# Stick-breaking attention with the keys in even and odd pairs: a scan over pairs, and the subtraction ahead of GpSimd's product

## The chip, the cores and the metric

One core of a Trainium2 chip runs the whole kernel. Its engines are TensorE (PE in the profile, PEld for its weight loads), VectorE (DVE), ScalarE (ACT), GpSimd (POOL) and SyncE (SP, which issues the DMAs here). Each has a queue of its own and they wait for each other by semaphores. The metric is the device time in microseconds of one execution; lower is better.

## The reference

A decoder layer on 2048 tokens of width 1024, in float32. The change touches the eight stick-breaking heads of 64 dimensions:

```python
for start in range(0, S, Q_BLOCK):
    end = start + Q_BLOCK
    z = jnp.einsum('bhqd,bhkd->bhqk', q[:, :, start:end], k[:, :, :end]).astype(jnp.float32) * scale
    past = jnp.arange(end)[None, :] < jnp.arange(start, end)[:, None]
    log_beta = jax.nn.log_sigmoid(z)
    log_1m = jnp.where(past, jax.nn.log_sigmoid(-z), 0.0)
    acc = lax.cumsum(log_1m, axis=3, reverse=True) - log_1m
    w = jnp.where(past, jnp.exp(log_beta + acc), 0.0)
    outs.append(jnp.einsum('bhqk,bhkd->bhqd', w.astype(v.dtype), v[:, :, :end]))
```

So the weight of key s for query t is sigmoid(z[t,s]) times the product of (1 - sigmoid(z[t,j])) over the keys j between s and t. Beside them stand four differential heads (two softmax maps each), an output projection, and a SwiGLU feed-forward layer.

## The kernel before

The kernel has three stretches: the norm of the input and the first projections (to 75 us), the attention heads with the projections of later heads between them (to 1400 us, the stick-breaking ones to about 838), and the feed-forward layer. Matmuls take their operands as a high and a low half in float16, so that most products are three matmuls.

The stick-breaking heads are worked in four groups g of two heads h. For each group, `units_sb` goes over eight pairs of query blocks s (256 queries, as two blocks a of 128 on the partitions), and for each over chunks c of 512 keys, from the diagonal one backwards, and the two heads h: 160 units in all. The first chunk of each s is diagonal, with 256 or 512 keys (32 units of each size); the other 96 units have 512 keys. `W` is a unit's number of keys.

One unit (`unit_sb`): `scores` puts z for both a into PSUM (tile `psum`, two places of 1024 floats that take turns). In `main`, ACT writes `be`, the sigmoid of z, to SBUF (L736), and then 1 - beta, the sigmoid of -z, over z in PSUM (L737). DVE runs a product from the last key to the first over it, one scan for each a, into `gp` (L742); it starts at 2^14 on the diagonal and elsewhere at the first element of the `gp` of the chunk before, that is `cx[h]`. One small reduce (L746) copies that start value to the end of `gp`; on the diagonal a memset (L741) puts it there. POOL then multiplies `be` by `gp` shifted by one key (L754, on the diagonal L751): these are the weights. Two units later ACT casts them to float16 (`high`, tile `wh`, L762), three units later DVE subtracts to get the low half (`low`, tile `wl`, L769), both are turned by DMA transposes, and five units after the h = 1 unit `values` multiplies with V.

The main loop sets the order, by a clock of ticks, one tick for each unit:

```python
for kind in ("", "main", "mid", None):
    main() if kind == "main" else clock.run(kind)
```

What is due under "" runs ahead of the unit's `main` (here: `low` of the unit three before, and `values`), "mid" behind it (the evacuations of projections, `evac_q`, `evac_k`, `evac_v`), and None takes the rest ("hi": the casts of ACT). `look_ahead` then issues the next unit's scores and `fill_next` a piece of a projection.

`be`, `gp` and other tiles come from one ring of seven buffers (`ppp`, by `ptile`): a new tile takes the place of the one seven allocations ago and its first writer waits for that one's last reader. Before, each unit takes two, `gp` and then `be`.

Of the kernel before, what the change touches and what calls it, by code (L numbers as in the profile page):

```python
# [64 lines left out]
def hybrid_layer_kernel(  # L65
# [6 lines left out]
    nc = tc.nc  # L72
# [152 lines left out]
    with ExitStack() as actx:  # L225
# [49 lines left out]
        def ptile(name):  # L275
            return ppp.tile([128, 1026], F32, tag="pp", name=name)

# [3 lines left out]
        def transposed(wh, w):  # L281
# [3 lines left out]

        lam_t = rtp.tile([128, 1024], F32, tag="rt", name="lam_t")[:, 0:256].rearrange(
            "p (i d) -> p i d", i=4)
        subg = small("subg", bufs=1)

        def load_constants():  # L290
            nc.gpsimd.dma_start(out=mask_b, in_=mask_in.rearrange("m p k -> p m k"))
            for i, l in enumerate((lambda_q1, lambda_k1, lambda_q2, lambda_k2)):
                nc.sync.dma_start(out=lam_t[:, i, :], in_=l.to_broadcast([128, 64]))
            nc.sync.dma_start(out=subg, in_=diff_subln_g.rearrange("o p -> p o"))
            nc.sync.dma_start(out=qkg[:, 0, :], in_=diff_q_norm_g.to_broadcast([128, 64]))
            nc.sync.dma_start(out=qkg[:, 1, :], in_=diff_k_norm_g.to_broadcast([128, 64]))
# [196 lines left out]

        def stack(ps, dst, ts):

            for a, m in ((0, 0), (64, 1)):
                nc.scalar.activation(dst[a:a + 64, m, ts], ps[a:a + 64, :], AF.Copy, scale=OUT_SC)
            for a, m in ((0, 0), (64, 1)):
                nc.vector.scalar_tensor_tensor(dst[64 - a:128 - a, m, ts], ps[a:a + 64, :], OUT_SC,
                                               dst[a:a + 64, m, ts], ALU.mult, ALU.subtract)  # L500

        def evac_q(ps, q, ts):
            stack(ps, q[:, 0], ts)
            if ts.stop == 512:
                clock.at(1, lambda: swap(q))
# [4 lines left out]

        evac_k = stack

        def project_sb(c, g):
# [7 lines left out]
            for w2, ev, dst in ((ws[0], evac_q, q), (ws[1], evac_k, k)):  # L521
                for u in range(2):
                    yield from bank_totals()
                    ps = pj_tile("pj")
                    ts = slice(u * 256, u * 256 + 256)
# [6 lines left out]
                    clock.at(1, lambda ps=ps, ev=ev, dst=dst, ts=ts: ev(ps, dst, ts), "mid")  # L532
# [180 lines left out]
        def unit_sb(g, s, c, h, cx, step):  # L713
# [3 lines left out]
            u = {}  # L717

            def scores():
                need(g, cd)  # L720
                q, k = qkv[g][cd][0], qkv[g][c][1]
                z = u["z"] = place("z", 1024).rearrange("p (a n) -> p a n", a=2)
                for a in range(2):
                    qs = o + a * 128
                    for y in range(2):
                        mm(z[:, a, 0:W], q[:, y, h, qs:qs + 128], k[:, h, 0:W], y == 0,
                           y == 1 and not diag)
                    if diag:
                        mm(z[:, a, qs:qs + 128], ident_b, mask_b[:, 0, :], False, True)

            def main():
                z, sc = u["z"], scl[g]
                gp = ptile("gp").rearrange("p (a n) -> p a n", a=2)
                be = ptile("be")[:, 0:2 * W].rearrange("p (a n) -> p a n", a=2)

                nc.scalar.activation(be, z[:, :, 0:W], AF.Sigmoid, scale=sc[:, 0:1])  # L736
                nc.scalar.activation(z[:, :, 0:W], z[:, :, 0:W], AF.Sigmoid, scale=sc[:, 1:2])  # L737
                for a in range(2):
                    e = o + (a + 1) * 128 if diag else 512
                    if diag:  # L740
                        nc.vector.memset(gp[:, a, e:e + 1], 2.0 ** 14)  # L741
                    nc.vector.tensor_tensor_scan(  # L742
                        gp[:, a, 0:e][:, ::-1], z[:, a, 0:e][:, ::-1], be[:, a, 0:e][:, ::-1],
                        2.0 ** 14 if diag else cx[h][:, a, 0:1], ALU.mult, ALU.bypass)
                if not diag:
                    nc.vector.tensor_reduce(gp[:, :, 512], cx[h][:, :, 0:1], axis=AX.X, op=ALU.max)  # L746
                cx[h] = gp
                if diag:
                    for a in range(2):
                        e = o + (a + 1) * 128  # L750
                        nc.gpsimd.tensor_mul(be[:, a, 0:e], be[:, a, 0:e], gp[:, a, 1:e + 1])  # L751
                    nc.gpsimd.memset(be[:, 0, o + 128:W], 0.0)
                else:
                    nc.gpsimd.tensor_mul(be, be, gp[:, :, 1:513])  # L754

# [3 lines left out]
                def high():  # L759
                    wh = u["wh"] = htile("wh")[:, 0:n]  # L760
                    if True:
                        nc.scalar.copy(wh, b2)  # L762
# [49 lines left out]
        def unit_diff(g, i, m, j, cx):  # L812
# [6 lines left out]
            def scores():  # L819
# [4 lines left out]
                for o in range(b, e, 512):  # L824
# [887 lines left out]
```

## Time and profile before

| | |
|---|---|
| time of the runs, median of 3 | 2962.2 us (2958.57 to 2964.27) |
| the profiled execution's own time | 2957.14 us |
| its span | 2955.1 us |
| mean TensorE clock granted | 0.948 |
| busy: PE, DVE, ACT, POOL | 2578.5, 2465.3, 1534.1, 1482.8 us |

A row of a group gives the line, the engine, the operation, output and inputs by the program's names, the shape, and the count; then the busy time in us and the mean of one in ns; then the idle time of the engine just before these instructions, and who ended most of it. A row of a timeline gives the start and the duration in us. A row of the waits gives who waited for whom, the sum in us, how often, and the longest.

### The profile page before, as it was taken

Reading aid. Unit: us, or ns where it says so; the run is one execution under the profiler, and the core shown is the slowest. Engines: PE = TensorE matmul, PEld = TensorE weight load, DVE = VectorE, ACT = ScalarE, POOL = GpSimd, SP = SyncE. Lnnn points to the kernel's source line nnn. Section 1 sums busy time; section 2 is a strip of 40 time slices with the busy share of each in tenths; the row PEclk is TensorE's granted clock in tenths of the full one; section 3 lists DMA queues with packets and bytes.
Section 4 is the critical chain, followed back from the end, with each engine's and each line's share of the span. In section 5 each row is a group of like instructions: output and inputs, shape, how many; then the busy total and the mean of one; then the engine's idle time right before and its main releaser. Section 6 shows DMA issues by size and latency. Waiting matters only on the chain.

```text
span 2955.1 us, 51682 instructions
## 1 busy us (share of the span) xinstructions
PE 2578.5 (87%) x20076; PEld 1587.4 (54%) x20076; DVE 2465.3 (83%) x3653; ACT 1534.1 (52%) x2539; POOL 1482.8 (50%) x1259
## 2 busy tenths in 40 slices
PE   7867778879678687786899899989999999999999
PEld 6646556657466576675674344444444444444444
DVE  7998999999988889989756788889877776777776
ACT  6776777777545565555534545454444343334332
POOL 2453455455757757666313455655454444444442
PEclk8989989989889899997999999999999999999999
DMA  4565667677655545567865412231116432112111
GB/s 162 103 130 107 123 128 130 124 127 133 108 99 95 93 97 98 108 117 154 178 158 142 136 58 79 84 113 68 43 62 127 138 102 86 43 43 78 52 43 72
DMA packets 736790, 305.80 MB, mean 103 GB/s; under 512 B 619296, under 2 KB 713760, under 8 KB 736544
## 3 DMA queue, kind: packets, MB, share of 16 engines
q1 hardware_dynamic: 736272, 302.43, 45.3%
q8 instruction: 157, 2.57, 0.4%
q14 instruction: 89, 0.73, 0.1%
q0 software_dynamic: 272, 0.07, 0.0%
HBM read 127.34 MB, written 28.31 MB: 53 GB/s over the span
## 4 chain that ended last, share of the span: by engine, by line
PE 47%; DVE 28%; issue 9%; POOL 5%; ACT 5%; DMA 4%; SPq 1%; DVEq 0%; ACTq 0%; POOLq 0%
PE pw L167 32%; PE psum L167 14%; DVE gp L742 4%; DVE wl L769 4%; DVE mx L178 2%; DVE fs L1296 2%; DVE acc_a L1569 2%; DMA wt<-wl 2%; DVE pt L178 1%; DVE hh L1348 1%; DVE wmx L105 1%; DMA wt<-al 1%; DVE rt L638 1%; DVE ws L161 1%; POOL sc L1486 1%
## 5 line engine op out<-in xcount | busy, mean ns | idle before, releaser
L167 PE MATMUL pw<-t,fs 128*128 128x512 f16 x3696 | 805.5, 380 | 12.3 <-ACT fs L1295 3.8
L167 PEld LDWEIGHTS <-fs 128*128 128x128 f16 x3696 | 359.6, 98 | 449.2 <-issue 6.8
L167 PE MATMUL psum<-k,q 128*128 128x512 f16 (+3 forms) x1280 | 339.8, 375 | 211.6 <-DVE gp L742 75.6
L167 PE MATMUL pw<-acc_b,at 128*128 128x512 f16 x2112 | 465.2, 380 | 19.4 <-DVE cg L1494 8.5
L167 PE MATMUL psum<-ws,h_hi 128*128 128x128 f16 x4096 | 386.4, 227 | 20.1 <-ACT psum L928 10.7
L167 PE MATMUL psum<-ws,h_lo 128*128 128x128 f16 x2048 | 374.7, 226 | 0.0
L167 PEld LDWEIGHTS <-h_hi 128*128 128x128 f16 x4096 | 336.3, 102 | 48.6 <-issue 29.7
L167 PEld LDWEIGHTS <-at 128*128 128x128 f16 x2112 | 206.1, 98 | 270.5 <-issue 26.5
L754 POOL TENSOR_TENSOR be<-be,gp 128x1024 f32<-128x1024 f32 x96 | 215.1, 2241 | 261.6 <-DVE gp L746 217.1
L167 PEld LDWEIGHTS <-q 128*128 128x128 f16 x1280 | 117.5, 100 | 329.9 <-issue 276.6
L1497 POOL TENSOR_TENSOR cg<-cg,cu 128x512 f32<-128x512 f32 x88 | 112.1, 1274 | 360.5 <-ACT cg L1496 341.0
L1569 DVE SCALAR_TENSOR_TENSOR acc_a<-pw,isd,acc_a 128x512 f32<-128x512 f32 x352 | 248.5, 744 | 49.3 <-PE pw L167 48.9
L1295 ACT ACTIVATE fs<-acc_b,fst 128x512 f16<-128x512 f32 x264 | 175.9, 713 | 211.2 <-POOL acc_b L1284 145.3
L1296 DVE SCALAR_TENSOR_TENSOR fs<-acc_b,fst,fs 128x512 f16<-128x512 f32 x264 | 248.3, 980 | 33.2 <-ACT fs L1295 33.1
L1486 POOL TENSOR_TENSOR sc<-sc 128x512 f32<-128x512 f32 x132 | 219.4, 1679 | 88.8 <-ACT sc L1480 88.8
L769 DVE TENSOR_TENSOR wl<-be,wh 128x1024 f16<-128x1024 f32 (+1 forms) x160 | 259.3, 1621 | 4.8 <-DMA wt<-wl 3.2
L742 DVE TENSOR_TENSOR_SCAN gp<-psum,gp,be 128x512 f32<-128x512 f32 x192 | 235.2, 1265 | 2.2 <-ACT psum L737 1.4
L736 ACT ACTIVATE be<-psum,gsc 128x1024 f32<-128x1024 f32 (+1 forms) x160 | 164.7, 1029 | 133.1 <-DVE wl L769 55.5
L167 PEld LDWEIGHTS <-h_lo 128*128 128x128 f16 x2048 | 209.3, 102 | 0.0
L1480 ACT COPY sc<-pw 128x512 f32<-128x512 f32 x176 | 100.1, 581 | 208.5 <-PE pw L167 184.7
L854 ACT ACTIVATE pt<-psum,nb,ds_sc 128x1024 f32<-128x1024 f32 (+4 forms) x192 | 183.0, 954 | 22.0 <-DVE pt L178 8.0
L178 DVE TENSOR_REDUCE mx<-psum 128x1 f32<-128x1024 f32 (+4 forms) x192 | 173.7, 905 | 24.1 <-PE psum L167 20.1
(222 smaller groups left out, 4850.2 us busy)
## 6 DMA issues: line engine op xcount, KB each, us to landing
acc_b<-in_w_gate_dram SPq DMA_DIRECT2D x22, 1024.0 KB, 5.2
acc_b<-in_w_up_dram SPq DMA_DIRECT2D x22, 1024.0 KB, 7.3
acc_b<-in_w_down_dram SPq DMA_DIRECT2D x22, 1024.0 KB, 9.1
raw<-in_w_in_dram SPq DMA_DIRECT2D x24, 512.0 KB, 4.6
xt<-in_x_dram SPq DMA_DIRECT2D x16, 512.0 KB, 5.2
raw<-in_w_o_dram SPq DMA_DIRECT2D x16, 512.0 KB, 4.2
mt<-mix_d SPq DMA_DIRECT2D x32, 256.0 KB, 3.5
out_dram<-acc_a SPq DMA_DIRECT2D x16, 512.0 KB, 2.9
```

The costliest lines, as they stand in the source:

```text
L167: nc.tensor.matmul(ps, lhsT=lhsT, rhs=rhs, start=start, stop=stop)
L178: fn(*a, **k)
L736: nc.scalar.activation(be, z[:, :, 0:W], AF.Sigmoid, scale=sc[:, 0:1])
L742: nc.vector.tensor_tensor_scan(gp[:, a, 0:e][:, ::-1], z[:, a, 0:e][:, ::-1], be[:, a, 0:e][:, ::-1], 2.0 ** 14 if diag else cx[h][:, a, 0 ...
L754: nc.gpsimd.tensor_mul(be, be, gp[:, :, 1:513])
L769: nc.vector.tensor_sub(wl, b2, u["wh"])
L854: nc.scalar.activation(pt, u["z"][:, 0:e - b], AF.Exp, scale=ds_sc, bias=nb[:, m:m + 1], accum_out=su[:, jj:jj + 1])
L1295: nc.scalar.activation(w[:, m, 0:4], src, AF.Copy, scale=sw)
L1296: nc.vector.scalar_tensor_tensor(w[:, m, 4:8], src, sw, w[:, m, 0:4], ALU.mult, ALU.subtract)
L1486: nc.gpsimd.tensor_add(s[m], s[m], y[m])
L1497: nc.gpsimd.tensor_mul(g, g, u)
L1569: nc.vector.scalar_tensor_tensor(acc[:, i, hs], ps, pr.isd, acc[:, i, hs], ALU.mult, ALU.add)
```

## The change

K's columns and V's tokens are stored so that in each chunk all even keys come first and then all odd ones (P = W/2 of each). The product of (1 - beta) over a pair is one step of a scan over P pairs, whose two multiplications take the even factor and the odd one. ACT now writes the even half of 1 - beta to `gp` in SBUF and the odd half over z in PSUM; the scan works in place in `gp`, which then holds the product at each pair's even key. For the even keys' weights the odd key's factor is still missing, so DVE multiplies the even half of `be` by the odd factors (a new instruction). POOL's product takes `gp` shifted by one pair, for both halves alike. `gp` is one buffer for the units of both heads (three allocations for two units instead of four). `low` of the unit three before gets the kind "low" and runs inside `main`, after the new product and before the reduce or memset that POOL waits for. Diagonal units work on their whole width, with masked scores giving 0 and 1, where before scans and products stopped at the diagonal and a memset on POOL cleared the rest.

```diff
         def evac_k(ps, k, u):
+            stack(ps.rearrange("p (n r) -> p r n", r=2),
+                  by_parity(k)[:, :, :, u * 128:u * 128 + 128])
...
-                    ts = slice(c * 512 + (2 * u + j) * 128, c * 512 + (2 * u + j + 1) * 128)
+                    ts = slice(c * 512 + u * 256 + j, c * 512 + u * 256 + 256, 2)
...
                     for y in range(2):
-                        mm(z[:, a, 0:W], q[:, y, h, qs:qs + 128], k[:, h, 0:W], y == 0,
+                        mm(za, q[:, y, h, qs:qs + 128], k[:, h, :, 0:P], y == 0,
                            y == 1 and not diag)
                     if diag:
-                        mm(z[:, a, qs:qs + 128], ident_b, mask_b[:, 0, :], False, True)
+                        n = 128 - 64 * a
+                        mm(za[:, :, P - n:P], ident_b, mask_p[:, :, 0:n], False, True)
 
             def main():
                 z, sc = u["z"], scl[g]
-                gp = ptile("gp").rearrange("p (a n) -> p a n", a=2)
+                if h == 0:
+                    step["gp"] = ptile("gp").rearrange("p (h a n) -> p h a n", h=2, a=2)
+                gp = step["gp"][:, h]
                 be = ptile("be")[:, 0:2 * W].rearrange("p (a n) -> p a n", a=2)
                 nc.scalar.activation(be, z[:, :, 0:W], AF.Sigmoid, scale=sc[:, 0:1])
-                nc.scalar.activation(z[:, :, 0:W], z[:, :, 0:W], AF.Sigmoid, scale=sc[:, 1:2])
+                nc.scalar.activation(gp[:, :, 0:P], z[:, :, 0:P], AF.Sigmoid, scale=sc[:, 1:2])
+                nc.scalar.activation(z[:, :, P:W], z[:, :, P:W], AF.Sigmoid, scale=sc[:, 1:2])
                 for a in range(2):
-                    e = o + (a + 1) * 128 if diag else 512
-                    if diag:
-                        nc.vector.memset(gp[:, a, e:e + 1], 2.0 ** 14)
+                    ga = gp[:, a, 0:P][:, ::-1]
                     nc.vector.tensor_tensor_scan(
-                        gp[:, a, 0:e][:, ::-1], z[:, a, 0:e][:, ::-1], be[:, a, 0:e][:, ::-1],
-                        2.0 ** 14 if diag else cx[h][:, a, 0:1], ALU.mult, ALU.bypass)
-                if not diag:
-                    nc.vector.tensor_reduce(gp[:, :, 512], cx[h][:, :, 0:1], axis=AX.X, op=ALU.max)
+                        ga, ga, z[:, a, P:W][:, ::-1],
+                        2.0 ** 14 if diag else cx[h][:, a, 0:1], ALU.mult, ALU.mult)
+                nc.vector.tensor_mul(be[:, :, 0:P], be[:, :, 0:P], z[:, :, P:W])
+                clock.run("low")
+                if diag:
+                    nc.vector.memset(gp[:, :, P:P + 1], 2.0 ** 14)
+                else:
+                    nc.vector.tensor_reduce(gp[:, :, P], cx[h][:, :, 0:1], axis=AX.X, op=ALU.max)
                 cx[h] = gp
-                if diag:
-                    for a in range(2):
-                        e = o + (a + 1) * 128
-                        nc.gpsimd.tensor_mul(be[:, a, 0:e], be[:, a, 0:e], gp[:, a, 1:e + 1])
-                    nc.gpsimd.memset(be[:, 0, o + 128:W], 0.0)
-                else:
-                    nc.gpsimd.tensor_mul(be, be, gp[:, :, 1:513])
+                b4 = be.rearrange("p a (r n) -> p a r n", r=2)
+                nc.gpsimd.tensor_mul(b4, b4, gp[:, :, 1:P + 1].rearrange(
+                    "p a (r n) -> p a r n", r=1).to_broadcast([128, 2, 2, P]))
...
-                clock.at(3, low, "")
+                clock.at(3, low, "low")
...
-                               v[:, kb, x, hh * 64:(hh + 1) * 64],
+                               v[:, vb, x, hh * 64:(hh + 1) * 64],
```

The mask is built anew: its diagonal part goes by an SP load and two DVE instructions into `mask_p`, even and odd columns apart; the differential heads keep theirs as `mask_b`.

How instructions then stand on DVE in two full units of the second group of heads (`gp`, `be`, `wh` and `wl` with the numbers of their buffers, so that the same unit can be found again; `q` and `k` are projections being evacuated; what the rows call SCALAR_TENSOR_TENSOR on `gp` are the scans, one for each a). Before:

```order
L742 SCALAR_TENSOR_TENSOR gp_2813<-psum_122,gp_2666,be_2814 128x512 x2
L746 TENSOR_REDUCE gp_2813<-gp_2666 128x2
L499 SCALAR_TENSOR_TENSOR q_2779<-psum_122,q_2779 64x256 x2
L769 TENSOR_TENSOR wl_2882<-be_2667,wh_2825 128x1024
L161 SCALAR_TENSOR_TENSOR ws_2373<-raw_2371,wsw_2660,ws_2373 128x1024
L742 SCALAR_TENSOR_TENSOR gp_2887<-psum_122,gp_2761,be_2888 128x512 x2
L746 TENSOR_REDUCE gp_2887<-gp_2761 128x2
L499 SCALAR_TENSOR_TENSOR q_2779<-psum_122,q_2779 64x256 x2
L769 TENSOR_TENSOR wl_2931<-be_2762,wh_2899 128x1024
```

The same two units in the changed kernel:

```order
L760 SCALAR_TENSOR_TENSOR gp_2764<-gp_2764,gp_2642,psum_122 128x256 x2
L763 TENSOR_TENSOR be_2818<-be_2818,psum_122 128x2x256
L784 TENSOR_TENSOR wl_2825<-be_2643,wh_2780 128x1024
L768 TENSOR_REDUCE gp_2764<-gp_2642 128x2
L505 SCALAR_TENSOR_TENSOR q_2788<-psum_122,q_2788 64x256 x2
L161 SCALAR_TENSOR_TENSOR ws_2373<-raw_2371,wsw_2669,ws_2373 128x1024
L760 SCALAR_TENSOR_TENSOR gp_2893<-gp_2893,gp_2764,psum_122 128x256 x2
L763 TENSOR_TENSOR be_2894<-be_2894,psum_122 128x2x256
L784 TENSOR_TENSOR wl_2901<-be_2671,wh_2835 128x1024
L768 TENSOR_REDUCE gp_2893<-gp_2764 128x2
```

The subtraction into `wl` has moved from behind the reduce and the evacuation to a place between the scans and the reduce, the scans are half as long, and the product into `be` is new.

On ACT, the second of these units before and after (`ws` is a weight being split; a row's brackets name the engines or DMA queues whose semaphores it waits for). Before:

```order
L762 CAST wh_2825<-be_2667 128x1024 [waits DMAHW6_49,Pool_49]
L157 ACTIVATE ws_2373<-raw_2371,wsw_2660 128x1024 [waits DMAHW0_49,DVE_49]
L736 ACTIVATE be_2888<-psum_122,gsc_136 128x1024 [waits PE_49,Activation_49]
L737 ACTIVATE psum_122<-psum_122,gsc_136 128x1024
L497 ACTIVATE q_2779<-psum_122 64x256 [waits PE_49]
```

After, with the unit that follows it (h = 1):

```order
L779 CAST wh_2835<-be_2671 128x1024 [waits DMAHW7_49,DVE_49,Pool_49]
L157 ACTIVATE ws_2373<-raw_2371,wsw_2669 128x1024 [waits DVE_49]
L755 ACTIVATE be_2894<-psum_122,gsc_137 128x1024 [waits PE_49]
L756 ACTIVATE gp_2893<-psum_122,gsc_137 128x2x256 [waits DVE_49]
L757 ACTIVATE psum_122<-psum_122,gsc_137 128x2x256 [waits Activation_49]
L503 ACTIVATE q_2788<-psum_122 64x256 [waits PE_49]
L503 ACTIVATE q_2788<-psum_122 64x256
L779 CAST wh_2911<-be_2765 128x1024 [waits DMAHW1_49,Pool_49]
L755 ACTIVATE be_2948<-psum_122,gsc_137 128x1024 [waits DVE_49,PE_49]
L756 ACTIVATE gp_2893<-psum_122,gsc_137 128x2x256
L757 ACTIVATE psum_122<-psum_122,gsc_137 128x2x256 [waits Activation_49]
```

There are three sigmoids for a unit instead of two. The even half of the h = 0 unit (`gp_2893`) waits for DVE, namely for `wl_2825` of the unit just before, which reads `be_2643`, the buffer that `gp_2893` takes; the odd half waits for ACT itself to end the even half.

More of the change, by code (lines that the diff above doesn't have):

```diff
@@ L266, in hybrid_layer_kernel @@
         ident_b = ac.tile([128, 128], BF16, name="ident_b")
-        mask_b = ac.tile([128, 2, 128], BF16, name="mask_b")
+        mask_b = ac.tile([128, 128], BF16, name="mask_b")
+        mask_p = ac.tile([128, 2, 128], BF16, name="mask_p")
         nlam = ac.tile([128, 1], F32, name="nlam")
@@ L275, in ptile @@
         def ptile(name):
-            return ppp.tile([128, 1026], F32, tag="pp", name=name)
+            return ppp.tile([128, 1028], F32, tag="pp", name=name)
         def htile(name):
@@ L284, in transposed @@
             return wt
-        lam_t = rtp.tile([128, 1024], F32, tag="rt", name="lam_t")[:, 0:256].rearrange(
-            "p (i d) -> p i d", i=4)
+        lam_t = rtp.tile([128, 1024], F32, tag="rt", name="lam_t")
+        mask_t = lam_t[:, 256:384]
+        lam_t = lam_t[:, 0:256].rearrange("p (i d) -> p i d", i=4)
         subg = small("subg", bufs=1)
         def load_constants():
-            nc.gpsimd.dma_start(out=mask_b, in_=mask_in.rearrange("m p k -> p m k"))
+            nc.gpsimd.dma_start(out=mask_b, in_=mask_in[1])
+            nc.sync.dma_start(out=mask_t, in_=mask_in[0])
             for i, l in enumerate((lambda_q1, lambda_k1, lambda_q2, lambda_k2)):
@@ L299, in constants @@
             nc.vector.tensor_copy(ident_b, ident)
+            nc.vector.memset(mask_p[:, :, 64:128], -(2.0 ** 120))
+            nc.vector.tensor_copy(mask_p[:, :, 0:64], mask_t.rearrange("p (n r) -> p r n", r=2))
             lam_s = small("lam_s", 2, bufs=1)
@@ L492, in weights, with stack, evac_q @@
                     yield END
-        def stack(ps, dst, ts):
+        def stack(ps, dst):
             for a, m in ((0, 0), (64, 1)):
-                nc.scalar.activation(dst[a:a + 64, m, ts], ps[a:a + 64, :], AF.Copy, scale=OUT_SC)
+                nc.scalar.activation(dst[a:a + 64, m], ps[a:a + 64], AF.Copy, scale=OUT_SC)
             for a, m in ((0, 0), (64, 1)):
[L499 to L504, printed above, removed]
+                nc.vector.scalar_tensor_tensor(dst[64 - a:128 - a, m], ps[a:a + 64], OUT_SC,
+                                               dst[a:a + 64, m], ALU.mult, ALU.subtract)
+        def evac_q(ps, q, u):
+            stack(ps, q[:, 0, :, u * 256:u * 256 + 256])
+            if u == 1:
                 clock.at(1, lambda: swap(q))
@@ L509, in swap, with by_parity, evac_k @@
                 nc.sync.dma_start(out=q[64 - a:128 - a, 1], in_=q[a:a + 64, 0])
-        evac_k = stack
+        def by_parity(k):
+            return k.rearrange("p m (r n) -> p m r n", r=2)
+        def evac_k(ps, k, u):
+            stack(ps.rearrange("p (n r) -> p r n", r=2),
+                  by_parity(k)[:, :, :, u * 128:u * 128 + 128])
         def project_sb(c, g):
@@ L524, in project_sb @@
                     ps = pj_tile("pj")
-                    ts = slice(u * 256, u * 256 + 256)
                     hs = slice(c * 512 + u * 256, c * 512 + u * 256 + 256)
@@ L717, in unit_sb @@
             u = {}
+            P = W // 2
             def scores():
                 need(g, cd)
-                q, k = qkv[g][cd][0], qkv[g][c][1]
+                q, k = qkv[g][cd][0], by_parity(qkv[g][c][1])
                 z = u["z"] = place("z", 1024).rearrange("p (a n) -> p a n", a=2)
@@ L800, in store @@
                 clock.at(1, lambda: store_mix(g, s * 256, 256, st))
-            return scores, None, main, W, 4 * W + 3 * W + (128 if diag else 0) * 2
+            return scores, None, main, W, 4 * W + 3 * W + (384 if diag else 0)
         def units_diff(g):
```

11 lines of the change are left out of this document (5 added, 6 removed).

## The prediction

> **What bounds the kernel now.** I read the page's head, then the busy time of one stretch, then the groups by form inside it, then the timeline of two units.
>
> ```profile
> span 2955.1 us, 51682 instructions
> ...
> DVE  7998999999988889989756788889877776777776
> ```
>
> The slices say that DVE (VectorE) is nearly always busy from the second slice to about the eleventh of 74 us each. That is where the stick-breaking units lie, by the lines of their first and last instruction:
>
> ```profile
> L742 DVE TENSOR_TENSOR_SCAN gp<-psum,be x128: 409/814/1220, 77.9 to 784.4; 128x128 f32<-128x128 f32 x32, 128x256 f32<-128x256 f32 x32, 128x384 f32<-128x384 f32 x32, 128x512 f32<-128x512 f32 x32
> L769 DVE TENSOR_TENSOR wl<-be,wh x160: 666/1226/3017, 85.2 to 838.2; 128x1024 f16<-128x1024 f32 x128, 128x512 f16<-128x512 f32 x32
> ```
>
> From 77.9 to 838 us, then; of what the diff touches, only the name of a mask is used later.
>
> ```profile
> core 0: us, PE busy (x) PEld busy (x) DVE busy (x) ACT busy (x) POOL busy (x), PEclk, DMA share, GB/s
> 75.00:833.00 758.00, 591.44 (x6038) 439.06 (x6038) 728.88 (x1026) 529.74 (x682) 380.39 (x316) 0.91 0.66 122
> ```
>
> In these 758 us DVE works 728.9: it is the bound, with 29 us to spare. PE (TensorE) has 591, ACT (ScalarE) 530, POOL (GpSimd) 380. So what DVE saves there shortens the kernel, until PE's 591 or a chain through ACT takes over. Who waits for whom agrees (the second row is the scores' group in this stretch):
>
> ```profile
> ACT be L736 <- DVE wl L769: 55.5, 35, 4.3
> L167 PE MATMUL psum<-k,q 128*128 128x512 f16 (+2 forms) x640 | 182.8, 385 | 135.9 <-DVE gp L742 75.6 <-DVE gp L746 28.9 <-DVE gp L741 28.0
> ```
>
> PE's 136 us ahead of the scores are waits for DVE to free a score buffer. What DVE spends on the 160 units (96 full ones of 512 keys against an earlier block, 32 diagonal ones of 512 and 32 of 256):
>
> ```profile
> L742 DVE TENSOR_TENSOR_SCAN gp<-psum,gp,be 128x512 f32<-128x512 f32 x192 | 235.2, 1265 | 2.2 <-ACT psum L737 1.4
> L742 DVE TENSOR_TENSOR_SCAN gp<-psum,be 128x512 f32<-128x512 f32 x32 | 38.9, 1214 | 0.0
> L742 DVE TENSOR_TENSOR_SCAN gp<-psum,be 128x384 f32<-128x384 f32 x32 | 30.4, 949 | 4.3 <-ACT psum L737 4.1
> L742 DVE TENSOR_TENSOR_SCAN gp<-psum,be 128x256 f32<-128x256 f32 x32 | 21.8, 682 | 0.0
> L742 DVE TENSOR_TENSOR_SCAN gp<-psum,be 128x128 f32<-128x128 f32 x32 | 13.4, 419 | 6.5 <-ACT psum L737 5.7
> L769 DVE TENSOR_TENSOR wl<-be,wh 128x1024 f16<-128x1024 f32 x128 | 220.0, 1719 | 4.3 <-DMA wt<-wl 3.2
> L769 DVE TENSOR_TENSOR wl<-be,wh 128x512 f16<-128x512 f32 x32 | 39.3, 1227 | 0.5
> L746 DVE TENSOR_REDUCE gp<-gp 128x2 f32<-128x2 f32 x96 | 12.3, 128 | 0.0
> L741 DVE MEMSET gp<- 128x1 f32 x128 | 7.6, 59 | 0.0
> ```
>
> Scans 339.7 us, the subtraction (`wl`) 259.3, reduces and memsets 19.9: 618.9. The other 110 us are evacuations of projections and weight work, 0.69 per unit. The subtraction's mean of 1.72 us mixes two cases, which the timeline shows (first DVE, then POOL, then ACT, of one stretch):
>
> ```profile
> 607.25 0.41 DVE L549 SCALAR_TENSOR_TENSOR v<-psum,v 128x256 f16<-128x256 f32 x1
> 607.59 2.98 DVE L769 TENSOR_TENSOR wl<-be,wh 128x1024 f16<-128x1024 f32 x1
> ...
> 614.05 0.12 DVE L746 TENSOR_REDUCE gp<-gp 128x2 f32<-128x2 f32 x1
> 614.09 1.21 DVE L769 TENSOR_TENSOR wl<-be,wh 128x1024 f16<-128x1024 f32 x1
> 615.23 2.45 DVE L742 TENSOR_TENSOR_SCAN gp<-psum,gp,be 128x512 f32<-128x512 f32 x2
> 617.60 0.12 DVE L746 TENSOR_REDUCE gp<-gp 128x2 f32<-128x2 f32 x1
> 617.64 1.21 DVE L769 TENSOR_TENSOR wl<-be,wh 128x1024 f16<-128x1024 f32 x1
> 618.77 2.45 DVE L742 TENSOR_TENSOR_SCAN gp<-psum,gp,be 128x512 f32<-128x512 f32 x2
> ```
> ```profile
> 607.48 2.00 POOL L754 TENSOR_TENSOR be<-be,gp 128x1024 f32<-128x1024 f32 x1 [3.96 <-DVE gp L746]
> 614.34 2.82 POOL L754 TENSOR_TENSOR be<-be,gp 128x1024 f32<-128x1024 f32 x1 [4.86 <-DVE gp L746]
> ```
> ```profile
> 615.40 1.11 ACT L736 ACTIVATE be<-psum,gsc 128x1024 f32<-128x1024 f32 x1 [1.69 <-DVE wl L769]
> ```
>
> The reduce lets POOL's product go, 0.2 us later. Where DVE starts the subtraction at once (614.09) it takes 1.21 us and POOL's product is stretched from 2.00 to 2.82. Where an evacuation comes between (607.25), POOL is first and the subtraction takes 2.98. So a unit with nothing beside it lasts 3.54 us (615.23 to 618.77), all DVE, and the other kind pays 1.77 more.
>
> **The change, by its parts.** *Scans.* Each covers half the elements: 256 in 64 diagonal scans and in the 192 of full units, 128 in 64. By the rows 682 ns, 682 + 51 (1265 less 1214, the price of a start value from memory) = 733, and 419: 43.6 + 140.7 + 26.8 = 211.1 us instead of 339.7, **-128.6**. This takes the second multiplication in the loop as free; between 128 and 512 elements the rows give (1214 - 419)/384 = 2.07 ns for an element. No row has a scan with two real operations. From below it can't be cheaper; from above I let it cost half a loop more, 1.04 ns, which is 256 x 0.265 + 64 x 0.133 = +76. I take 0, since today's row already pays twice what a plain product does per element (0.8 to 1.0 ns, below), and keep 76 as a rival.
>
> *A new product* on DVE, `be` (SBUF) by the odd half of the scores' buffer (PSUM), 512 elements in 128 units, 256 in 32. Nearest rows, of the same mix of memories:
>
> ```profile
> L1494 DVE TENSOR_TENSOR cg<-pw,sc 128x512 f32<-128x512 f32 x88 | 60.2, 684 | 29.2 <-POOL sc L1486 29.2
> L1018 DVE SCALAR_TENSOR_TENSOR acc_b<-psum,iso,acc_b 128x256 f32<-128x256 f32 x32 | 14.8, 481 | 21.4 <-PE psum L167 16.8 <-ACT psum L928 4.6
> ```
>
> 128 x 0.684 + 32 x 0.481 = **+103**. *The subtraction* now stands after the product and ahead of the reduce or memset that POOL waits for, so POOL has at that time only the product of the unit before, begun 0.2 us after that unit's reduce and 2.0 long. DVE reaches the subtraction two scans and a product later (1.4 + 0.65) if nothing lies between: a wait of 0.15 at most. At 1.21 and, by the shortest of the small form, about 0.67 us: 128 x 1.21 + 32 x 0.67 = 176.3, **-83**. Its ends are 0 (POOL still in the way) and -83. POOL starts 1.2 us later in a unit; its reader, the cast `wh`, comes two units on, so that is hidden. *Memsets:* 64 fewer, -3.8. Together **-112** on DVE.
>
> *ACT.* The second sigmoid becomes two, the even half into `gp`, the odd one in place and waiting for the first to end. Rows:
>
> ```profile
> L736 ACT ACTIVATE be<-psum,gsc 128x1024 f32<-128x1024 f32 x128 | 142.7, 1115 | 106.2 <-DVE wl L769 55.5 <-PE psum L167 30.4 <-POOL be L754 10.1
> L737 ACT ACTIVATE psum<-psum,gsc 128x1024 f32<-128x1024 f32 x128 | 138.6, 1083 | 0.0
> L736 ACT ACTIVATE be<-psum,gsc 128x512 f32<-128x512 f32 x32 | 22.0, 688 | 26.8 <-POOL be L754 8.8 <-PE psum L136 8.3 <-PE psum L167 7.7
> L737 ACT ACTIVATE psum<-psum,gsc 128x512 f32<-128x512 f32 x32 | 21.0, 655 | 0.0
> L762 ACT CAST wh<-be 128x1024 f16<-128x1024 f32 x128 | 133.8, 1045 | 38.0 <-DMA wt<-wh 16.4 <-DVE wl L769 12.0 <-POOL be L754 4.4
> ```
>
> 0.688 + 0.655 against 1.083: 0.26 more in 128 units, about 0.2 in 32, +40 on an engine with 228 us idle; hidden by itself. But `gp` is now ACT's output, one buffer for the two units h = 0, 1, and by the order on ACT the even half of an h = 0 unit waits for DVE's `wl` of the unit just before (its buffer is the `be` that this `wl` reads). Before, `be` too waited for a `wl` (the 55.5 us), but with two scans left to hide behind. Now: `wl` ends, 0.1 until ACT starts (615.30 to 615.40), 0.69, 0.655, 0.1 again, then the scan: 1.55 us in which DVE has the reduce (0.12) and the 0.69 of evacuations and weight work, which come unevenly (none at 614 us, 0.41 at 607); I take half the gaps as empty and half as full. A mean hole of (1.43 + 0.05)/2 = 0.74 in 64 pairs, about half that in the 16 small ones: 47 + 6 = **+53** given back. Its ends: 64 x 1.43 + 16 x 1.0 = +108, if evacuations wait too, and +10, if every gap has work. The h = 1 unit has no such wait: ACT goes on with `wh`, `be` and the halves, 3.5 us by the rows and some 3.3 with neighbours overlapping, against 3.1 on DVE (two scans, product, subtraction, reduce, also overlapping): +0.2 where no evacuation stands, +8 in 40 pairs. Against that, instructions overlap by 0.08 (the reduce lasts 0.12, and the next starts 0.04 after it) and there is one more in a unit: -13. Net **-5**.
>
> *PE.* Scores, values and projections keep their columns; masks gain 64 x 128 columns, hidden. V's tokens are taken at a step of two, so its 16 x 96 weight loads read `h` with a step. None of the rows has a strided load:
>
> ```profile
> L167 PEld LDWEIGHTS <-h_hi x1472: 95/98/152, 98.5 to 823.5; 128*128 128x128 f16 x184
> ```
>
> Ends: 0, and a load of twice the 98 ns, 1536 x 0.098 = 150 us on PE, of which 136 stand idle now. I take 0. *K's evacuation* reads PSUM at a step of two:
>
> ```profile
> L499 DVE SCALAR_TENSOR_TENSOR k<-psum,k 64x256 f16<-64x256 f32 x64 | 27.0, 422 | 3.8 <-ACT k L497 2.4
> ```
>
> Ends: 0, and twice the streamed part, (684 - 422)/256 = 1.02 ns x 256 x 64 = +17 on DVE. I take 0, the contiguous row being the only one. [...] *POOL's* broadcast product costs no more than a plain one in the nearest rows (256 elements):
>
> ```profile
> L640 POOL TENSOR_TENSOR st<-st,cs 128x256 f32<-128x256 f32 x32 | 28.5, 891 | 2.5
> L751 POOL TENSOR_TENSOR be<-be,gp 128x256 f32<-128x256 f32 x32 | 26.7, 834 | 3.7 <-DVE gp L742 2.6 <-DVE gp L741 0.2
> ```
>
> 7% of 2.0 us is 0.14, on an engine half idle. One more 64 KB load on SP and two small DVE operations in the first 75 us: under 1 us.
>
> **Sum:** -112 + 53 - 5 = -64, with 2 for leftover waits of `wl`: **-62 us**. Against the profiled execution's own time (2957.1, of which 2955.1 are its span) that is 2895; that execution is 5 below the median of the runs, 2962.2, so I forecast **2900**.
>
> **The rivals.**
> 1. *ACT and PE hold more of it.* PE's 591 us are 3.7 a unit on average, against 4.35 that DVE would then take (696/160), and where projection blocks stand close together PE is above its mean; holes add up when engines are this close. For: the stretch shrinks to 696 us under PE's 591. Against: that leaves 105 us of idle PE. With the hole at 1.2 instead of 0.74 (+32 on 64 to 80 pairs): 2935. Chance 0.17.
> 2. *The holes are filled,* evacuations falling where ACT is awaited: 53 becomes 13, 2860. Chance 0.13.
> 3. *Slower: the scan pays for its second multiplication.* +76: 2976. It decides from about 0.24 us for a 256-element scan (62 us over 256). For: its loop must now go through two multiplications. Against: 2.07 ns an element today, where the new product's neighbour needs (684 - 481)/256 = 0.8, so the loop already has a spare step. Chance 0.08. [...]
> 4. *Slower or no gain: the turn doesn't come,* POOL still holding the subtraction back, if its product grows past 3 us: the 83 stay, 2983. Chance 0.05.
> 5. *Strided weight loads at double price,* 591 + 150 = 741 us of PE in a stretch of now 758: the gain is all but eaten, 2950. For: no load here has a step. Against: nothing but that the bytes loaded are as many. Chance 0.07.
> 6. *K's read at a step at full price:* +17, 2917; it lies in the forecast's own range and 0.10 of its 0.50.
>
> **How the numbers follow.** The forecast has 0.50, with its own range 2875 to 2925. Runs of this kernel lie 5.7 us apart, so 0.2% (6 us) is about what can be told from nothing. The range takes in rival 2 and 1, K's 17 and the edge of 5, and leaves out 3 and 4 and some tails: 2852 to 2965. Faster: 0.50 + 0.13 + 0.15 of rival 1 + 0.03 of rival 5 = 0.81; no change 0.05; slower 0.14.
>
> **What would show it.** Right: 256-element scans at 0.73 us, the product at 0.68, `wl` of 1024 at 1.21 with hardly a row over 1.5, POOL's product at 2.0, and DVE idle ahead of every second unit's scan, released by ACT's odd-half sigmoid, some 50 us in all; the stretch near 696 us. Wrong: scans near 1.0 us (rival 3), `wl` still at 2 to 3 (4), loads from `h_hi` near 0.2 (5), or the hole ahead of scans near 100 us. Past 840 us nothing should move.

## The result and the profile after

The changed kernel takes 2926.98 us (median of 4 runs, 2924.35 to 2931.6) against 2960.39 before; the ratio is 0.9889 with a 95% interval of 0.987 to 0.9909. So it is faster by 33 us, where 62 were forecast, and the time lies 2 us past the end of the forecast's own range (2875 to 2925). In a later set of runs it gave 2927.99 and a ratio of 0.9898 (0.9881 to 0.9914).

The head of the page and DVE's row of the slices, after:

```profile
span 2929.8 us, 51760 instructions
...
DVE  8887888888988898899757788889877776776776
```

Almost all the nines of the first eleven slices have become eights: DVE is no longer always busy there. One row each for the stretch of the stick-breaking units, from the first scan to the last transpose of a `wl`, before and after (length, then busy time of PE, PEld, DVE, ACT and POOL):

```profile
77.90:839.50 761.60, 594.71 (x6066) 442.14 (x6065) 731.23 (x1032) 531.30 (x687) 385.16 (x318) 0.90 0.66 123
```
```profile
78.50:812.30 733.80, 591.77 (x6074) 442.45 (x6073) 623.19 (x1129) 570.95 (x847) 358.21 (x190) 0.90 0.70 127
```

DVE has 108 us less to do, and its idle time has grown from 30 (761.60 - 731.23) to 111 (733.80 - 623.19): of 108 us, 80 turned into waiting, and the stretch is 28 shorter. The rest of the gain in the medians is within what runs differ by: the profiled run, at 2931.6, is the slowest of the four.

The groups inside the stretch, after: DVE's first, then ACT's two halves and POOL's product.

```profile
L760 DVE TENSOR_TENSOR_SCAN gp<-gp,psum 128x256 f32<-128x256 f32 x256 | 173.3, 718 | 75.7 <-ACT psum L757 71.3 <-PE psum L167 2.8
L784 DVE TENSOR_TENSOR wl<-be,wh 128x1024 f16<-128x1024 f32 x128 | 163.7, 1279 | 2.4 <-ACT v L560 1.9 <-DMA wt<-wl 0.4
L756 ACT ACTIVATE gp<-psum,gsc 128x512 f32<-128x512 f32 x128 | 87.7, 685 | 37.5 <-DVE wl L784 37.5
L757 ACT ACTIVATE psum<-psum,gsc 128x512 f32<-128x512 f32 x128 | 84.7, 662 | 4.2
L763 DVE TENSOR_TENSOR be<-be,psum 128x512 f32<-128x512 f32 x128 | 84.7, 662 | 0.0
L771 POOL TENSOR_TENSOR be<-be,gp 128x512 f32<-128x512 f32 x32 | 37.8, 1182 | 83.1 <-DVE gp L766 68.5 <-ACT gp L756 4.2 <-ACT st L594 3.3
L760 DVE TENSOR_TENSOR_SCAN gp<-gp,psum 128x128 f32<-128x128 f32 x64 | 23.4, 407 | 12.6 <-ACT psum L757 11.5 <-PE psum L167 0.6
L784 DVE TENSOR_TENSOR wl<-be,wh 128x512 f16<-128x512 f32 x32 | 22.8, 713 | 0.0
L763 DVE TENSOR_TENSOR be<-be,psum 128x256 f32<-128x256 f32 x32 | 12.6, 395 | 0.0
```

The durations are near the forecast: scans 173.3 + 23.4 = 196.7 us, product 97.3, subtraction 186.5. What has grown is the idle time ahead of the scans, 75.7 + 12.6 us where the forecast's rows have 2.2 + 4.3 + 6.5. The waits of the stretch, after (who waits for whom, us, times, longest):

```profile
DVE gp L760 <- ACT psum L757: 82.8, 84, 3.7
PE psum L167 <- DMA wt<-wl: 64.0, 45, 5.0
ACT gp L756 <- DVE wl L784: 47.5, 38, 4.6
ACT wh L779 <- DMA wt<-wh: 26.8, 23, 3.0
ACT be L755 <- PE psum L167: 25.1, 25, 2.3
```

and the same first two before:

```profile
DVE gp L742 <- ACT psum L737: 11.2, 10, 3.4
...
PE psum L167 <- DMA wt<-wl: 10.5, 10, 3.7
```

Scans wait for the odd half of ACT (83 us instead of 11), and new beside it is PE's wait for the transposes of `wl` (64 instead of 10.5). Three holes within 12 us of each other, the first from a chain that began 10 us earlier, show three different causes. DVE, SP's queue, PE and ACT, after:

```profile
592.01 1.22 DVE L784 TENSOR_TENSOR wl<-be,wh 128x1024 f16<-128x1024 f32 x1
...
603.98 1.39 DVE L760 TENSOR_TENSOR_SCAN gp<-gp,psum 128x256 f32<-128x256 f32 x2 [1.71 <-ACT psum L757]
605.28 0.66 DVE L763 TENSOR_TENSOR be<-be,psum 128x512 f32<-128x512 f32 x1
605.86 1.22 DVE L784 TENSOR_TENSOR wl<-be,wh 128x1024 f16<-128x1024 f32 x1
606.99 0.15 DVE L768 TENSOR_REDUCE gp<-gp 128x2 f32<-128x2 f32 x1
608.10 0.73 DVE L760 TENSOR_TENSOR_SCAN gp<-gp,psum 128x128 f32<-128x128 f32 x2 [0.96 <-ACT psum L757]
...
615.11 1.26 DVE L760 TENSOR_TENSOR_SCAN gp<-gp,psum 128x256 f32<-128x256 f32 x2 [2.01 <-ACT psum L757]
```
```profile
593.30 1.25 SPq L285 DMA_TRANSPOSE wt<-wl  x1
...
607.15 1.25 SPq L285 DMA_TRANSPOSE wt<-wl  x1
608.49 1.28 SPq L285 DMA_TRANSPOSE wt<-wh  x1
```
```profile
597.20 2.50 PE L167 MATMUL psum<-wt,v 128*64 128x256 f16 x21 [3.40 <-DMA wt<-wl]
599.63 2.31 PE L167 MATMUL psum<-k,q 128*128 128x512 f16 x6
```
```profile
601.56 1.11 ACT L755 ACTIVATE be<-psum,gsc 128x1024 f32<-128x1024 f32 x1 [2.21 <-PE psum L167]
...
603.87 1.03 ACT L779 CAST wh<-be 128x1024 f16<-128x1024 f32 x1
...
607.11 0.47 ACT L756 ACTIVATE gp<-psum,gsc 128x256 f32<-128x256 f32 x1 [1.62 <-DVE wl L784]
...
611.75 1.04 ACT L779 CAST wh<-be 128x1024 f16<-128x1024 f32 x1 [1.28 <-DMA wt<-wh]
```

- *Hole at 603.98, late scores.* `wl` ends at 593.23, its transpose is issued at 593.30, and PE's `values` wait for it until 597.20. The next scores stand behind them (599.63), ACT waits for the scores until 601.56, and DVE has nothing for 1.71 us.
- *Hole at 608.10, the buffer.* ACT's even half waits until `wl` of the unit before has ended at 607.08, whose `be` it overwrites. This is the hand-off of the forecast. It does not come in every pair: the ring's buffers are not handed out strictly in turn, and by the program's addresses `gp` takes the `be` of the unit four before (five allocations ago, not seven) in 47 of 80 pairs; the even half waits for its subtraction in 46.
- *Hole at 615.11, the cast.* `wh` of 603.87 ends at 604.90, but SP turns it only at 608.49, behind the transpose of a `wl` that ends at 607.08. `wh` and `wl` take turns in four buffers, so the cast two units on, at 611.75, waits for that transpose to end, and the sigmoids stand behind the cast.

Followed back in this way from every hole, 25 to 30 us lie behind the buffer wait, as much behind late scores, 10 behind casts, 6 where ACT simply had work, and the rest in small pieces.

### The profile page after: what moved, and what is told of

It reads as the page before. It is cut to its first block, busy times and chain, and to the rows that moved or that the text cites. A ratio compares the mean times of both kernels' runs of the same rounds, so it can differ in the third digit from the quotient of the medians.

```text
span 2929.8 us, 51760 instructions
## 1 busy us (share of the span) xinstructions
PE 2577.5 (88%) x20076; PEld 1586.6 (54%) x20076; DVE 2356.7 (80%) x3751; ACT 1573.7 (54%) x2699; POOL 1454.3 (50%) x1131
## 4 chain that ended last, share of the span: by engine, by line
PE 49%; DVE 23%; ACT 7%; DMA 7%; POOL 6%; issue 6%; SPq 1%; DVEq 0%; ACTq 0%; POOLq 0%
PE pw L167 32%; PE psum L167 16%; DMA wt<-wl 4%; DVE gp L760 2%; DVE wl L784 2%; DVE fs L1313 2%; DVE acc_a L1586 2%; DVE mx L178 2%; DVE pt L178 1%; DVE be L763 1%; DVE hh L1365 1%; DMA wt<-al 1%; ACT be L755 1%; ACT gp L756 1%; DVE ws L161 1%
## 5 line engine op out<-in xcount | busy, mean ns | idle before, releaser
L771 POOL TENSOR_TENSOR be<-be,gp 128x1024 f32<-128x1024 f32 (+1 forms) x160 | 320.3, 2002 | 378.9 <-DVE gp L768 208.8
L167 PE MATMUL psum<-k,q 128*128 128x512 f16 (+3 forms) x1280 | 331.9, 377 | 132.1 <-ACT pt L871 75.8
L167 PE MATMUL psum<-ws,h_hi 128*128 128x128 f16 x4096 | 384.2, 226 | 21.8 <-ACT psum L945 11.6
L760 DVE TENSOR_TENSOR_SCAN gp<-gp,psum 128x256 f32<-128x256 f32 (+1 forms) x320 | 196.6, 656 | 88.2 <-ACT psum L757 82.8
L167 PE MATMUL psum<-wt,v 128*64 128x256 f16 x1728 | 141.2, 300 | 74.0 <-DMA wt<-wl 64.0
L167 PE MATMUL psum<-h_hi,ws 128*128 128x256 f16 x1024 | 188.1, 280 | 5.3 <-DVE q L505 3.1
```

What stands on the lines that cost most here:

```text
L167: nc.tensor.matmul(ps, lhsT=lhsT, rhs=rhs, start=start, stop=stop)
L760: nc.vector.tensor_tensor_scan(ga, ga, z[:, a, P:W][:, ::-1], 2.0 ** 14 if diag else cx[h][:, a, 0:1], ALU.mult, ALU.mult)
L771: nc.gpsimd.tensor_mul(b4, b4, gp[:, :, 1:P + 1].rearrange("p a (r n) -> p a r n", r=1).to_broadcast([128, 2, 2, P]))
```

## The experiments

Theory A: the holes are the buffer wait (the forecast's). Theory B: the later subtraction makes its transposes late, so `values`, so the scores. Rival C: ACT is too loaded, and taking a wait away gives little. All were timed beside the kernel before, which took 2959.4 to 2961.6 us in the same sets of runs. The first four:

*A buffer of its own for `gp`* (the ring's seven buffers divided: two for `gp`, five for `be`):

```diff
+        gps = []
...
-                    step["gp"] = ptile("gp").rearrange("p (h a n) -> p h a n", h=2, a=2)
+                    if not gps:
+                        gps.extend(ptile("gp") for _ in range(2))
+                    gps.reverse()
+                    step["gp"] = gps[0].rearrange("p (h a n) -> p h a n", h=2, a=2)
```

> The changed kernel, but with two gp tiles of its own that take turns by pair of units (be has the other five buffers), so that ACT's even half of 1 - beta no longer takes the buffer that the subtraction of the unit just before still reads. Theory A (that buffer wait makes the holes ahead of the scans): ACT's waits of gp for wl (47.5 us, 38 times) go, DVE's waits for the odd half fall from 83 to about 50 us, the time falls by 20 to 30 us against the changed kernel's 2927, to about 2900 (ratio to the kernel before 0.978 to 0.982). Theory B (the later subtraction makes its transposes, the values and so the next scores late on PE): PE's waits for the transposes of wl stay at 60 us or grow, and the time falls by 10 at most, since the scores become the next thing to be late. Theory C (ACT is simply too loaded): the holes stay, below 5 us.

2918.5 us, 0.9864 (0.9842 to 0.9886): 8 less, as theory B had it (10 at most), not the 20 to 30 of theory A. The wait of `gp` for `wl` is gone and the holes fell by 19, to 64 us, but the subtraction grew by 10 us (196.4 instead of 186.5). DVE and POOL of this kernel show why:

```profile
175.88 0.72 DVE L765 TENSOR_TENSOR_SCAN gp<-gp,psum 128x128 f32<-128x128 f32 x2
176.51 0.39 DVE L768 TENSOR_TENSOR be<-be,psum 128x256 f32<-128x256 f32 x1
176.83 2.34 DVE L789 TENSOR_TENSOR wl<-be,wh 128x1024 f16<-128x1024 f32 x1
```
```profile
175.73 2.36 POOL L776 TENSOR_TENSOR be<-be,gp 128x1024 f32<-128x1024 f32 x1 [1.32 <-DVE wsw L140]
```

With no hole ahead of the short diagonal scans, DVE reaches the subtraction at 176.83, while POOL's product of the unit before lasts to 178.09, and is held until then: it takes 2.34 us, where the one at 170.96 takes 1.22. Subtractions over their plain length (1.22 us for 1024 elements, 0.68 for 512) by more than 0.15 us are 36 here and 22 in the changed kernel. Part of the hole had been waiting that the subtraction would otherwise have had to do.

*Scores ahead of the values* on PE:

```diff
+            if g < SBP and n + 1 < len(plan) and plan[n + 1][0] == g:
+                look_ahead(n)
             for kind in ("", "main", "mid", None):
```

> The changed kernel, but the next unit's scores are issued at the start of a tick, on PE ahead of the values that wait for the transposes of wl. Theory B: the scores no longer stand behind those waits, DVE's waits for the odd half fall from 83 to about 50 us and the time by 15 to 30 us, to about 2905 (ratio 0.979 to 0.984). Theory A: the holes of the buffer wait stay, so little changes, 0 to 10 us. Theory C: nothing. Against B too: the scores may stand in front of the queue waiting for their PSUM place, which DVE frees only after the product, and hold back projections; then the time is the same or up to 10 us longer.

2914.0 us, 0.9847 (0.983 to 0.9864): 13 less, between what theory A (0 to 10) and theory B (15 to 30) had. PE's wait for `wl` fell from 64 to 9.9 us, as theory B says; the holes only to 70, not to 50.

*Both:*

> Both edits, gp with two tiles of its own and the scores ahead of the values. If A and B each make about 30 of the 83 us of waits ahead of the scans, the two together bring 40 to 55 us against the changed kernel: 2870 to 2887 (ratio 0.970 to 0.975), with at most 30 us of such waits left. If only A or only B holds, it is as the better of the two alone. If C holds, within 10 us of the changed kernel.

2908.9 us, 0.9829 (0.9811 to 0.9847): 18 less than the changed kernel and not 40 to 55. What grew is ACT's wait of the cast, from 26.8 to 50.9 us, and of the holes that are left, 50 us, half (some 25) stand behind it:

```profile
ACT wh L784 <- DMA wt<-wh: 50.9, 49, 3.0
DVE gp L765 <- ACT psum L762: 49.6, 52, 2.6
```

So A and B both hold and neither is enough: a third wait takes their place.

*The old turn* (pairs stay, the subtraction goes back ahead of the sigmoids):

```diff
-                clock.at(3, low, "low")
+                clock.at(3, low, "")
```

> The changed kernel with the subtraction back at its old place, ahead of the unit's sigmoids and scans and behind the evacuations; pairs, product and shared gp stay. If the turn is worth what the wl rows say (1.21 instead of 1.72 us in 128 units, 0.71 instead of 1.23 in 32), wl takes some 70 us more of DVE. By theory B the earlier subtraction also takes PE's waits for its transposes back from 64 to some 10 us, by theory A the wait of gp for wl stays or shrinks. Net, if the turn's gain on DVE outweighs both: 2945 to 2960 (ratio 0.995 to 1.0), i.e. most of the change's gain comes from the turn. If the lateness costs as much as the turn brings: about 2927 again (0.989). If pairs alone are better: below 2920.

2944.3 us, 0.9951 (0.9937 to 0.9966), at the edge of what was expected. The subtraction takes 290 us, 31 more than in the kernel before and 104 more than in the changed one, and the holes are gone:

```profile
L784 DVE TENSOR_TENSOR wl<-be,wh 128x1024 f16<-128x1024 f32 x128 | 243.6, 1904 | 5.1 <-DMA wt<-wl 3.0 <-ACT gp L756 0.7 <-ACT wh L779 0.3
L784 DVE TENSOR_TENSOR wl<-be,wh 128x512 f16<-128x512 f32 x32 | 46.7, 1459 | 0.6 <-DMA wt<-wl 0.2
```
```profile
DVE gp L760 <- ACT psum L757: 12.3, 11, 3.8
```

Of the 104 us on DVE that the turn saves, the holes take back 70 (82.8 - 12.3): it brings 17. (DVE's whole busy time differs by 88, 711.7 in this stretch against 623.2, and the stretch by 15, 748.8 against 733.8.) PE's wait for `wl` is 15.7 us here, so it is indeed the turn that makes the transposes late.

*The turn without pairs* (the kernel before, with `low` run in `main` behind the scans, ahead of the reduce or memset):

```diff
+                clock.run("low")
                 if not diag:
                     nc.vector.tensor_reduce(gp[:, :, 512], cx[h][:, :, 0:1], axis=AX.X, op=ALU.max)
...
-                clock.at(3, low, "")
+                clock.at(3, low, "low")
```

> The kernel before, without pairs, with the turn alone: the subtraction runs inside the unit's main part, behind the two scans and ahead of the reduce or memset that lets GpSimd's product go. If the turn's gain on DVE is as in the changed kernel (wl 259 to 186 us) and its price (late transposes, holes ahead of scans) too, DVE's busy time in the stretch falls by some 70 us, and the time lies near 2940 to 2945 (ratio 0.993 to 0.995): pairs and turn then bring about half each of the changed kernel's 33 us. Rival: without pairs the wait of ACT for the subtraction falls on the first sigmoid, which has two scans of 1.26 us to hide behind, so the holes stay under 30 us and the turn alone brings as much as the whole change, 2920 to 2930. Against both: with 2.5 us of scans ahead of it the subtraction comes so late that PE's waits for its transposes eat the gain, 2955 or more.

3010.3 us, 1.0171 (1.0156 to 1.0186): 51 slower than before. The number falls under the expectation's last case (2955 or more), but not by its mechanism: PE's wait for transposes is 82.6 us, where the changed kernel has 64. The subtraction is quick, 182.6 us. But:

```profile
ACT be L736 <- DVE gp L745: 156.1, 63, 9.2
PE psum L167 <- DMA wt<-wl: 82.6, 51, 5.1
```
```profile
606.31 0.67 DVE L772 TENSOR_TENSOR wl<-be,wh 128x512 f16<-128x512 f32 x1
606.89 0.15 DVE L745 TENSOR_REDUCE gp<-gp 128x2 f32<-128x2 f32 x1
607.08 0.86 DVE L499 SCALAR_TENSOR_TENSOR q<-psum,q 64x256 f16<-64x256 f32 x2
609.27 2.46 DVE L740 TENSOR_TENSOR_SCAN gp<-psum,gp,be 128x512 f32<-128x512 f32 x2 [1.34 <-POOL be L757]
```
```profile
607.09 1.11 ACT L736 ACTIVATE be<-psum,gsc 128x1024 f32<-128x1024 f32 x1 [1.50 <-DVE gp L745]
608.11 1.08 ACT L737 ACTIVATE psum<-psum,gsc 128x1024 f32<-128x1024 f32 x1
```

The trace names the reduce, which ends at 607.04, but the semaphore for which `be` waits is that of the subtraction ahead of it, which ends at 606.98; so it is in all 63 of these waits. `be` takes the buffer of the `be` four units back, and its last reader is the subtraction that runs in the unit just before. In the kernel before it is the same (the 55.5 us of the forecast's row), but there that subtraction runs ahead of its unit's scans. Now it stands behind them; both sigmoids (2.1 us) come after it, and DVE has only the reduce and an evacuation in between. The expectation's rival had named this wait and let two scans hide it, but both stand ahead of the subtraction. The trace also puts the hole down to POOL, whose product (607.22 to 609.22) and ACT's sigmoid (to 609.19) end together. The product for which this scan waits is an earlier one, ended at 598.51, so it was the sigmoid that released the scan.

In the changed kernel three tiles serve two units, and `be` waits for a subtraction in no unit: only the even half of `gp` does, in 46 of 80 pairs, with the first sigmoid already done. So with pairs the turn gains, and without them it loses. This is read from the waits; no run gave the turn alone more buffers.

*The cast behind the sigmoids*, on top of the two edits:

```diff
                 nc.scalar.activation(z[:, :, P:W], z[:, :, P:W], AF.Sigmoid, scale=sc[:, 1:2])
+                clock.run("cast")
...
-                clock.at(2, high, "hi")
+                clock.at(3, high, "cast")
```

> The version with both edits (gp with two tiles of its own, scores ahead of the values), and besides the cast to wh moved on ACT from the end of a tick, ahead of the next unit's sigmoids, to behind them. Of the 51 us of holes ahead of scans that were left, 25.5 stand behind casts that wait for the transpose of an earlier wh. If that wait is the cause, the holes fall to some 25 us and the time by 12 to 25 us against the version with both edits (2909), to 2885 to 2897 (ratio 0.974 to 0.979). Rival: ACT is as full as DVE by then, the cast only moves its 1.05 us from ahead of this unit's sigmoids to ahead of the next one's, and the subtraction, which needs the cast, waits in its turn: no change, or slower by up to 10 us.

2874.9 us, 0.9715 (0.9695 to 0.9735), better than expected: 34 less than with two edits, 52 less than the changed kernel. It is the fastest version here.

```profile
DVE gp L766 <- ACT psum L762: 19.9, 23, 2.1
```
```profile
77.90:758.00 680.10, 569.32 (x6124) 430.98 (x6122) 632.96 (x1131) 566.13 (x853) 361.14 (x190) 0.94 0.77 137
```

The holes are down to 20 us and DVE is busy for 633 of 680 us. Rival C falls: ACT's 566 us were no bound. The control:

> The changed kernel itself once more, so that the others of this call can be compared with it on one chip: 2927 us, ratio 0.987 to 0.991.

2928.0 us, as told above. The cast alone, with `gp` of its own, and with the scores:

> The changed kernel with the move of the cast alone (behind the sigmoids of the unit three later; gp from the ring and the scores behind the values as in the changed kernel). By the walk back from its holes only some 10 of 86 us stand behind casts that wait for a transpose. If the waits are worth what the walk gives each of them, the time falls by 5 to 12 us against the changed kernel, to about 2918 (ratio 0.985 to 0.988). Rival: the wh transposes stand on SyncE's queue behind those of a wl that comes late, and the cast that waits for them in turn holds back all later sigmoids, so that the move is worth the 34 us that it brought on top of the other two edits: about 2895 (ratio 0.977 to 0.980).

> The changed kernel with gp in two tiles of its own and the move of the cast, but the scores behind the values as before. If PE's wait for late transposes of wl is worth about 10 us of holes whatever else stands, it is some 10 us slower than the version with all three edits (2875): 2882 to 2890 (ratio 0.973 to 0.977). Rival: with the sigmoids ahead of the casts ACT follows PE more closely and late scores tell more, 2895 to 2905 (ratio 0.978 to 0.982).

> The changed kernel with the scores ahead of the values and the cast behind the sigmoids, gp from the ring as in the changed kernel: the one combination of the three edits still missing. If the buffer wait of gp for wl is then the last thing that holds ACT back, as the forecast had it, the holes ahead of scans are 30 us or more by waits of gp for wl, and the time is 2895 to 2905 (ratio 0.978 to 0.982), 20 to 30 us above the version with all three. If that wait is worth the 5 to 8 us that its removal brought in the other combinations, it is 2880 to 2885 (ratio 0.973 to 0.975).

2910.2 us (0.9832, 0.9818 to 0.9845), 2901.9 (0.9804, 0.9791 to 0.9818) and 2885.2 (0.9747, 0.9734 to 0.9761). The first lies between its two theories; for the second the rival held, late scores tell more once the casts are out of the way (ACT waits 81.4 us for scores there, and 48.7 with the cast alone, instead of 25.1); for the third the small price of the buffer wait was right. All eight combinations (us; the four waits and the subtraction in the stretch):

| edits on the changed kernel | time | scan for ACT | gp for wl | PE for wl | cast for wh | wl busy |
|---|---|---|---|---|---|---|
| none | 2927.0 | 82.8 | 47.5 | 64.0 | 26.8 | 186.5 |
| gp | 2918.5 | 64.2 | - | 66.2 | 38.3 | 196.4 |
| scores | 2914.0 | 70.4 | 42.5 | 9.9 | 29.6 | 187.7 |
| cast | 2910.2 | 69.2 | 54.1 | 49.1 | 14.6 | 186.2 |
| gp, scores | 2908.9 | 49.6 | - | 11.0 | 50.9 | 197.1 |
| gp, cast | 2901.9 | 47.1 | - | 48.0 | 14.7 | 198.3 |
| scores, cast | 2885.2 | 44.7 | 53.1 | 10.9 | 14.5 | 187.9 |
| all three | 2874.9 | 19.9 | - | 11.0 | 15.2 | 201.3 |

Each edit cuts its own wait: `gp` to nothing, the scores to some 10 us, the cast to 15. The cast also takes PE's wait from 64 to 49 us, and with `gp` of its own the wait of the cast grows. `gp` brings 5 to 10 us in every company, because the subtraction takes back 9 to 13. Each time is known to 4 to 7 us to either side, so a single difference of 5 us can't be told from none; but all four of `gp` have one sign. The scores bring 10 to 13 without the cast and 25 to 27 with it; the cast 17 without the scores and 29 to 34 with them. ACT's sigmoids start when the last of buffer, scores and cast is there, so taking one away uncovers the next.

## Why the prediction was right or wrong, point by point

- *DVE's work: right by its parts, 17 us too good in all.* The sum had -112 and -13 for overlapping instructions, so -125; the busy time fell by 108. By the rows, scans -143.1 (339.7 to 196.6, forecast -128.6), product +97.3 (forecast +103), subtraction -72.8 (forecast -83), memsets -3.8, reduces +2.0; with 8.7 us more in another DVE instruction, the low halves of weights (21.8 to 30.5 in 14 of them), that is -111.7. The durations of scans came as forecast: 718 ns, where 682 and 733 give 720 for this mix, and 407 instead of 419. One by one they add up to 209.9 us; that DVE is busy for only 196.6 is the overlap of the two scans of a unit, which the forecast had as a term of its own. Durations of all DVE instructions exceeded its busy time by 55 us before and by 63 after: the overlap brought 8 us and not 13.
- *The subtraction's turn: right*, with a smaller size. The median is 1.218 us (forecast 1.21), but 22 of 160 still meet the tail of POOL's product, 8.5 us in all, where the forecast had none of that size (0.15 us at most for one). It took POOL's product as 2.0 us long and two full scans ahead of the subtraction; in the h = 1 units of 1024 elements the product takes 2.36 us (median; 2.34 at least), and 12 of the 22 follow the short scans.
- *The holes: this step failed, in kind more than in size.* The sum had +53 for the buffer wait, +8 for ACT and +2, together 63; DVE's idle time grew by 80, and the stretch came to 734 us instead of the forecast's 700 (762 - 62). So of the 34 us that are missing, 17 are idle time and 17 the work above. Ahead of the scans of h = 0 units DVE stands idle for 53 us, the forecast's number, but that is luck: by the walk back only 25 of them lie behind the buffer wait, which comes in 46 pairs and not in all 80. The other 33 us stand ahead of h = 1 units, 23 of them behind late scores. The buffer wait is real, but its removal brings 5 to 10 us. The part of the change on the turn asked what POOL does with a later start and who reads its product. It did not ask who waits for the new `wl`: its transpose on SP's queue, `values` on PE behind that and the next scores behind `values`; and in SP's order the transposes of `wh` behind those of `wl`, which hold the cast and with it ACT. These two waits cost nothing in the sum; taken away together they are worth 42 us (2927.0 to 2885.2), though the cast waited for its transposes before the change as well (row of `wh` in the forecast).
- *Rival 1 (ACT and PE hold more, 2935)* came nearest, but not by its mechanism: PE's 592 us had room, and it was late by waiting, not by load. *Rival 2* (holes filled by evacuations) did not come.
- *Rival 3 (dearer scan): refuted*, 718 ns for 256 elements, where the rows before give 720. *Rival 4 (no turn): refuted* by the median above. *Rivals 5 and 6 (strided loads, PSUM at a step): refuted*. V's loads with a step are among the first row's, K's evacuation is the second:

```profile
L167 PEld LDWEIGHTS <-h_hi x4096: 95/98/152, 48.7 to 1352.8; 128*128 128x128 f16 x196
```
```profile
L505 DVE SCALAR_TENSOR_TENSOR k<-psum,k 64x256 f16<-64x256 f32 x64 | 27.0, 422 | 3.9 <-ACT k L503 2.4
```

The longest load is 152 ns as before, and the evacuation, with its read of PSUM at a step of two, has its 422 ns to the nanosecond.

## What to carry to other kernels

When a step moves to a later place, follow its output as far as its buffers: who reads it, what stands behind that reader in its queue, and which later writer waits for the buffer, on SP's queue too. Where several waits end at one instruction, the wait that the profile names is only the last of them: in all twelve steps of the table its length was more than its removal brought, and the three gave 8, 13 and 17 us alone and 52 together. Which instruction released a wait is the profile's inference, too: where two of the same engine end close together, go by the buffer and its readers. Two parts of a change may need each other: pairs alone (with the shared `gp`) brought 15 us, the turn alone cost 51, both brought 33, because with pairs the first sigmoid no longer takes a buffer that the late subtraction still reads.

## What the runs showed of the hardware

A scan with two real multiplications, in place, cost no more here than the old one with one: 718 ns for 256 elements, where the old rows give 720 (682, and 51 more, 1265 less 1214, for a start value from memory in 192 of the 256), and 407 against 419 for 128. POOL's product of 1024 elements came in two lengths that alternate with the unit's head in this kernel, with medians of 2.00 and 2.36 us in 64 units each; in the kernel before it is 2.00 for both heads:

```profile
636.11 1.99 POOL L771 TENSOR_TENSOR be<-be,gp 128x1024 f32<-128x1024 f32 x1 [2.50 <-DVE gp L768]
640.70 2.37 POOL L771 TENSOR_TENSOR be<-be,gp 128x1024 f32<-128x1024 f32 x1 [2.60 <-DVE gp L768]
644.55 2.00 POOL L771 TENSOR_TENSOR be<-be,gp 128x1024 f32<-128x1024 f32 x1 [1.48 <-DVE gp L766]
```

The two differ in where their part of the shared `gp` tile starts; whether that is the cause was not tried.
